# Storing computed data from GpSimd, loading in program order in the last phases, and moving first sums and gate rows a little

## The chip, the cores and the metric

The kernel runs on one core of a Trainium2 chip. The time is the device time of one execution in microseconds (us), as the median of several runs. The core has five engines with instruction queues of their own: TensorE (PE: matmuls, and PEld for its weight loads), VectorE (DVE), ScalarE (ACT), GpSimd (POOL) and SyncE (SP). Each works its queue in order. A transfer (DMA) is started by an instruction in one engine's queue, which waits there until the data or the buffer it needs is ready; what stands behind it in that queue waits with it. The instructions themselves signal each other by semaphores.

## What is computed

One layer of a gated hybrid decoder for a prompt of 1024 tokens and 8 samples of 8 tokens, together 1088 rows. The model width is 1024, everything is float32.

```python
h = rmsnorm(x, norm_g) * (1.0 + scale[:, None]) + shift[:, None]     # shift, scale, gate = split(silu(c) @ ada_w + ada_b)
z = h @ w_in + b_in                                                   # one projection, 8456 columns, split below
ya, v_rows = chunk_gmlp(a_u, a_v, gmlp_vnorm_g, gmlp_ws, gmlp_bs)     # branch a: 128-position mixing in 4 channel groups
ya = ya * silu(a_g)
yb = swa_branch(b_q, b_k, b_v, ...) * silu(b_g)                       # branch b: attention over a window of 128
yc = mlstm_branch(c_qk, c_v, c_i, c_f, c_o, ...) * silu(c_g)          # branch c: mLSTM matrix memory, 4 heads
gates = sigmoid(m_g).reshape(bsz, t, 3, 1024)
merged = (gates[:, :, 0] * (ya @ w_branch_a)
          + gates[:, :, 1] * (yb @ w_branch_b)
          + gates[:, :, 2] * (yc @ w_branch_c))
x_out = x + gate[:, None] * (merged @ w_out)
```

It also returns the new key and value windows, the mLSTM states (C, n, m, the convolution's last rows) and the normed values of the gMLP samples.

## The kernel before

Matmuls keep float32 precision by splitting each operand into a high part (a cast on ScalarE to the matmul's type) and a low part (the rest, a subtraction on VectorE), and adding three products: high by high, high by low, low by high. A weight tile is thus loaded by SP, cast on ScalarE (L1377), subtracted on VectorE (L1378), and then used; hh/hl, yh/yl and mh/ml are the high and low parts of h, of a branch's y and of the merged rows.

In time the kernel has these parts. Up to 60 us it loads x and forms h. Up to 364 us it computes branch c (projections, convolution, and per head the mLSTM). Up to 618 us it computes branch b (key and value tiles, then attention steps with other matmuls filled in between) and the gMLP's values and mixing. From 618 to 1118 us comes what is called the gate phase here: the list `items`, worked one after the other, each prepared five items ahead (LEAD = 5; to prepare is to load and split weights). Most items are one of seven products of a Strassen-like scheme (`seven`, order Q7 = 1, 6, 7, 5, 3, 2, 4), which forms four blocks of a 2 x 2 block product out of seven; each product has two banks (j = 0, 1) of 272 columns with twelve matmuls each, and `collect` adds the bank to running sums on VectorE (L1457 to L1492). First come the four groups of branch a's gMLP, with the rows of the adaLN gate (`gate_rows`) between them; then per branch (order a, c, b) four pairs of merge gates and, behind each pair, two projections (`proj`) of the branch's y by its weights. `proj` multiplies the gate's tanh by the bank (L1610), for the second and third branch adds what the branches before left in DRAM (`mprev`, loaded from dmg at L1608, added at L1612), and stores to dmg (L1616); the last branch's last two row blocks (f = 3, 7) stay on the chip. `y_load` (L1573 to L1575) brings a branch's y from DRAM (dy) in eight loads through a staging buffer of two halves, casting and splitting each; it is an item of its own ahead of the first `proj` of branches c and b. `gate_b` multiplies branch b's y by its gate through DRAM.

From 1118 us on, the output projection: gbc and gbs (the adaLN gate, from drow) and six merged row blocks (mgr, from dmg) are loaded, mgr is split, the columns of w_out are loaded in four parts by `wo_load`, and 36 tiles are computed, 128 rows by 256 columns each, four times nine, of which the ninth has the 64 sample rows. Each takes 24 matmuls, then on VectorE the product with the gate (L1747) and the sum with x (L1748; xr, loaded at L1729), and is stored (L1749).

The order of the work: a scheduler places each engine's instructions by a simulation with priorities (`tc.high_priority()`), except where a manual schedule is entered for an engine: there the queue has the order of the program text. PE is in manual order from the kv tiles' end on (L1309). In before, SP is ordered by the scheduler throughout, and nearly all transfers, loads and stores, stand in its queue; POOL computes 32 operations and issues no transfer.

Of the kernel before, what the change touches and what calls it, by code (L numbers as in the profile page):

```python
# [30 lines left out]
HC = HT // 2  # L31
# [8 lines left out]
def trunk_kernel(ctx: ExitStack, tc: tile.TileContext, I, O):  # L40
    nc = tc.nc
# [419 lines left out]
    with tc.tile_pool(name="cph", bufs=1, side="right", reuse_waits="tile") as c1:  # L461
# [48 lines left out]
        for s, hs in ((0, (2, 3)), (1, (0, 1))):  # L510
# [14 lines left out]
            if s == 0:  # L525
# [43 lines left out]
                V.tensor_tensor(mt, cum, MM, ALU.add)  # L569
                nc.sync.dma_start(O["m_p"].rearrange("a b h -> (a h) b"), mt[:, 1023:1024])  # L570
                nc.sync.dma_start(O["m_s"].rearrange("a b h -> (a h) b"), smpl(mt)[:, :, 8])
                mprev = c1.tile([4, 16], F32, name="mprev")
# [28 lines left out]
                scr = dp.tile([8, NT], F32, name="scr")  # L601
                nc.sync.dma_start(scr[0:4], nM)
                nc.sync.dma_start(scr[4:8], wi)
                for q in range(3):
# [21 lines left out]
        hn = [None] * 4  # L626

        def head(h):
# [44 lines left out]
            for g in range(3):  # L673
# [27 lines left out]
                else:  # L701
                    S.copy(num[:, 6:8], pn[:, 0:258].rearrange("p (i x) -> p i x", x=129))
                    S.copy(num[:64, 8], pn[:64, 258:387])
            nc.sync.dma_start(O["C_p"][0, 0, h], Cp[:, 0:128])
            V.tensor_copy(nst[:, 0, h:h + 1], Cp[:, 128:129])
# [13 lines left out]
            for b2 in range(2):  # L719
                bs_ = slice(4 * b2, 4 * b2 + 4)  # L720
                V.tensor_tensor(Cs[b2], Cs[b2], dec[:, bs_].broadcast_to([128, 4, 129]), ALU.mult)
                V.tensor_tensor(vhm[:, bs_], vs.bitcast(F32).unsqueeze(1).broadcast_to([128, 4, 128]),
                                bmask[:, bs_].unsqueeze(2).broadcast_to([128, 4, 128]), ALU.mult)
                vlm = c1.tile([64, 4, 128], F32R, tag="kwm", bufs=2, name="vlm")
                V.tensor_tensor(vlm, vl.unsqueeze(1).broadcast_to([64, 4, 128]),
                                bmask[:64, bs_].unsqueeze(2).broadcast_to([64, 4, 128]), ALU.mult)
                pu = pk()
                mm(pu, kws, vhm[:, bs_].rearrange("p b e -> p (b e)"), True, False)
                mm(pu, kws[:64], vlm.rearrange("p b e -> p (b e)"), False, True)
                V.tensor_tensor(Cs[b2][:, :, 0:128], Cs[b2][:, :, 0:128], pu.rearrange("p (b e) -> p b e", b=4), ALU.add)  # L730
                V.tensor_tensor(Cs[b2][:, :, 128:129], Cs[b2][:, :, 128:129], un[:, bs_].unsqueeze(2), ALU.add)
                nc.sync.dma_start(O["C_s"][0, bs_, h].rearrange("b d e -> d b e"), Cs[b2][:, :, 0:128])
                V.tensor_copy(nst[:, 1 + 4 * b2:5 + 4 * b2, h:h + 1], Cs[b2][:, :, 128:129])
# [45 lines left out]
        V.tensor_copy(nrowo, ps[0:36, 0:128])  # L779
        nc.sync.dma_start(O["n_p"].rearrange("a b h d -> (a b h) d"), nrowo[0:4])  # L780
        nc.sync.dma_start(O["n_s"].rearrange("a b h d -> (a b h) d"), nrowo[4:36])
        crow = c1.tile([27, 1024], F32, tag="acc", name="crow")
        for q in range(2):
# [3 lines left out]
            S.copy(crow[:, 512 * q:512 * q + 512], ps[0:27])  # L787
        nc.sync.dma_start(O["conv_p"].rearrange("a b j c -> (a b j) c"), crow[0:3])
        nc.sync.dma_start(O["conv_s"].rearrange("a b j c -> (a b j) c"), crow[3:27])

        for h in range(4):
# [17 lines left out]
            gemm_T(wview(hl, 0, 128, 1024), wview(hl, 1, 128, 1024), 8, hh, hlo, ev_g)  # L809
            nc.sync.dma_start(dy[0, h], hn[h])  # L810

# [19 lines left out]
    with tc.tile_pool(name="bph", bufs=1, side="right", reuse_waits="tile") as b1:  # L831
# [62 lines left out]
        def spatial(step):  # L894
            ps = pk()
            if step == 0:
# [3 lines left out]
                G.affine_select(WTp, WTp, [[0, 4], [1, 128]], ALU.is_ge, 0.0, base=0, channel_multiplier=-1)  # L900
                nc.sync.dma_start(dWT, WTp)
                return
# [4 lines left out]
            G.affine_select(WTq, WTq, [[0, 4], [8, 8], [0, 8]], ALU.is_ge, 0.0, base=7, channel_multiplier=-1)  # L907
            nc.sync.dma_start(dWs, WTq)


        for nm, src in (("swa_k_s", "cache_swa_k"), ("swa_v_s", "cache_swa_v")):
            nc.sync.dma_start(O[nm][0, :, 0:120].rearrange("b j g d -> b (j g d)"),
                              I[src][0, :, 8:128].rearrange("b j g d -> b (j g d)"))
# [22 lines left out]
        def k_norm(n0):  # L936
# [9 lines left out]
            if n0 == 6:  # L946
                kout = bt([128, 2, 2, 64], "kout", tag="QT", bufs=3)
                V.tensor_tensor(kout.rearrange("p a g d -> p (a g) d"), v[:, 2:6],
                                kgb.unsqueeze(1).broadcast_to([128, 4, 64]), ALU.mult)
                nc.sync.dma_start(O["swa_k_p"][0, 0], kout[:, 0])  # L950
                for b in range(8):
                    nc.sync.dma_start(O["swa_k_s"][0, b, 120:128], kout[8 * b:8 * b + 8, 1])
            V.tensor_tensor(v, v, kqg.unsqueeze(1).broadcast_to([128, 6, 64]), ALU.mult)
# [69 lines left out]
        class Prompt:  # L1023
# [57 lines left out]
            def v(self):  # L1081
                g, n = self.g, self.n
                pO = pu_()
                for w in range(0 if n > 0 else 1, 2):
                    for r in range(2):
# [3 lines left out]
                S.activation(o, pO[:, 0:256], AF.Copy, scale=0.5)  # L1089
                nc.sync.dma_start(dy[1, 2 * g:2 * g + 2, :, 128 * n:128 * n + 128].rearrange("f p t -> p f t"),  # L1090
                                  o.rearrange("p (f t) -> p f t", f=2))
# [5 lines left out]
        class Sample:  # L1097
# [59 lines left out]
            def y(self):  # L1157
# [6 lines left out]
                c0 = 1024 + 32 * self.bg  # L1164
                nc.sync.dma_start(dy[1, 2 * self.g:2 * self.g + 2, :, c0:c0 + 32].rearrange("f p t -> p f t"), o)

        bhl = {}

        def bg_chunk(f, ci):
# [5 lines left out]
            def ev_b(ci, c0, n, ps):  # L1175
# [4 lines left out]
                V.scalar_tensor_tensor(z, t, 1.0, z, ALU.add, ALU.mult)  # L1180
                nc.sync.dma_start(dsg[f, :, c0:c0 + n], z)

# [87 lines left out]
        def mix(g):  # L1270
# [16 lines left out]
            if g == 3:  # L1287
                nc.sync.dma_start(O["gmlp_v_s"][0].rearrange("b t (g c) -> (b t) g c", g=4), A["gvo"])

# [9 lines left out]
        for n in range(9):  # L1299
            kv_tile(hl, n)  # L1300
            if n in (3, 5):
                spatial((n - 3) // 2)
            if n in (1, 3, 5, 7):
                t_first(n // 2)
            if n % 3 == 2:
# [3 lines left out]
        pe.enter_context(tc.manual_schedule(engines={mybir.EngineType.PE}))  # L1309
        nc.sync.dma_start(O["swa_v_p"][0, 0], vB[:, 7])  # L1310
        for b in range(8):
            nc.sync.dma_start(O["swa_v_s"][0, b, 120:128], vB[8 * b:8 * b + 8, 8])
        done = set()
# [275 lines left out]
    def proj(n, f, Tt):  # L1589
# [5 lines left out]
        def run(t):  # L1595
            if n == 2 and f % 4 == 3:
                m_tiles(f)
            for h in range(2):
                for j in range(2):
# [13 lines left out]
                    if n == 2 and f % 4 == 3:  # L1613
                        m_split(f, c0, HC, x)
                    else:
                        nc.sync.dma_start(dmg[f, :, c0:c0 + HC], x)  # L1616

# [4 lines left out]
    def gate_rows(g):  # L1622
# [20 lines left out]
        def run2(_):  # L1643
# [3 lines left out]
            V.tensor_scalar(m, m, 0.5, None, ALU.mult)  # L1647
            nc.sync.dma_start(drow[:, 256 * g:256 * g + 256], m)

# [7 lines left out]
    items += [act(t_in_place, *((k,) for k in range(4)))] + it[0][:5] + it[1][:1] + it[0][5:]  # L1657
    rest = it[1][1:3] + [None] + it[1][3:4] + [None] + it[1][4:5] + [None] + it[1][5:6] + [None] + it[1][6:] + [None]
    rest += it[2][:1] + [None] + it[2][1:2] + [None] + it[2][2:3] + [None] + it[2][3:] + it[3]
    items += [x or gr.pop(0) for x in rest]  # L1660

    def gate_b(f, b):
# [6 lines left out]
        V.tensor_tensor(x, x, y, ALU.mult)  # L1669
        nc.sync.dma_start(dy[1, f, :, c], x)  # L1670

# [13 lines left out]
    def prepare(i):  # L1685
        if i < len(items) and i not in ready:
            with tc.high_priority():
                ready[i] = items[i][0]() if items[i][0] else None

    for i in range(LEAD):  # L1690
        prepare(i)
# [91 lines left out]
```

## Time and profile before

| | before |
|---|---|
| median of 3 runs | 1226.4 us (1224.79 to 1227.68) |
| profiled execution | 1225.66 us |
| its span in the trace | 1223.9 us |
| mean granted TensorE clock | 0.98 |
| branch c | about 60 to 364 us |
| branch b and gMLP mixing | about 364 to 618 us |
| gate phase | about 618 to 1118 us |
| output projection | about 1118 to 1224 us |

A row of the timeline has the start in us, the duration in us, the engine, the line of the kernel, the operation, out<-in with tile names, shapes and a count; in brackets stands how long the engine idled before it and what released it. SPq is SP's queue; its transfers show the time of the issue, not of the data's way. A row of the waits has who waited, for whom, the total in us, how often, and the longest. In a table by stage the columns are the window, its length, and the busy time and count of each engine, then PE's granted clock, the share of the DMA engines and GB/s.

### The profile page before, as it was taken

Reading aid. Unit: us, or ns where it says so; the run is one execution under the profiler, and the core shown is the slowest. Engines: PE = TensorE matmul, PEld = TensorE weight load, DVE = VectorE, ACT = ScalarE, POOL = GpSimd, SP = SyncE. Lnnn points to the kernel's source line nnn. Section 1 sums busy time; section 2 is a strip of 40 time slices with the busy share of each in tenths; the row PEclk is TensorE's granted clock in tenths of the full one; section 3 lists DMA queues with packets and bytes.
Section 4 is the critical chain, followed back from the end, with each engine's and each line's share of the span. In section 5 each row is a group of like instructions: output and inputs, shape, how many; then the busy total and the mean of one; then the engine's idle time right before and its main releaser. Section 6 shows DMA issues by size and latency. Waiting matters only on the chain.

```text
span 1223.9 us, 23322 instructions
## 1 busy us (share of the span) xinstructions
PE 1173.7 (96%) x8900; PEld 1124.1 (92%) x8900; DVE 820.3 (67%) x2146; ACT 485.8 (40%) x1215; POOL 17.8 (1%) x32
## 2 busy tenths in 40 slices
PE   5899999999979999999979999999999999999998
PEld 2689999999969998988878999999999999999998
DVE  4767878655568778886599885655766676668333
ACT  4443444433332266887234433333433342236000
POOL 1000000000001000000000000000000000000000
PEclk9999999999989999999979999999999999999999
DMA  9711222224122211211144246522633364466332
GB/s 328 242 47 36 72 74 70 76 86 126 54 58 67 56 40 44 67 38 59 55 119 118 75 120 201 161 80 84 177 112 110 110 171 125 126 197 190 95 91 83
DMA packets 155818, 129.76 MB, mean 106 GB/s; under 512 B 13551, under 2 KB 146311, under 8 KB 155690
## 3 DMA queue, kind: packets, MB, share of 16 engines
q1 hardware_dynamic: 155706, 128.27, 35.4%
q8 instruction: 70, 1.15, 0.4%
q14 instruction: 42, 0.34, 0.1%
HBM read 99.39 MB, written 29.82 MB: 106 GB/s over the span
## 4 chain that ended last, share of the span: by engine, by line
PE 88%; DVE 5%; SPq 3%; DMA 3%; ACT 1%; issue 1%; DVEq 0%
PE pg L85 48%; PE pk L85 23%; PE pu L85 14%; PE pk L89 2%; DMA raw<-in_w_in_dram 2%; SPq L256 1%; PE pu L89 1%; DMA xts<-in_x_sample_dram 1%; SPq L272 1%; DVE comb L1372 0%; DVE prod L1378 0%; DVE hl L125 0%; ACT hl L124 0%; DVE wo L1378 0%; DVE ml L1585 0%
## 5 line engine op out<-in xcount | busy, mean ns | idle before, releaser
L85 PE MATMUL pg<-hl,hl 128*128 128x256 f32 (+3 forms) x904 | 281.1, 311 | 0.0
L85 PE MATMUL pg<-hh,hl 128*128 128x384 f32 (+1 forms) x912 | 242.2, 340 | 1.1 <-DVE hh L399 1.1
L85 PE MATMUL pg<-hl,hh 128*128 128x256 f32 (+1 forms) x1008 | 182.9, 287 | 1.0 <-DVE zif L524 1.0
L85 PEld LDWEIGHTS pg<-hl,hl 128*128 128x128 f32 x904 | 172.1, 190 | 2.4 <-issue 1.9
L85 PEld LDWEIGHTS pg<-hh,hl 128*128 128x128 f32 x912 | 163.8, 191 | 5.3 <-DVE hh L399 2.2
L85 PEld LDWEIGHTS pg<-hl,hh 128*128 128x128 f32 x1008 | 152.9, 190 | 1.5 <-PE pg L85 1.1
L1377 ACT CAST prod<-raw 128x512 fp32r<-128x512 f32 x76 | 47.1, 620 | 125.7 <-PE pk L85 54.8
L85 PE MATMUL pg<-hh,prod 128*128 128x272 f32 x400 | 84.9, 292 | 6.8 <-ACT prod L1377 6.8
L85 PE MATMUL pk<-hh,prod 128*128 128x272 f32 x368 | 78.0, 291 | 0.0
L85 PEld LDWEIGHTS pg<-hh,prod 128*128 128x128 f32 x400 | 66.7, 191 | 7.3 <-ACT prod L1377 6.9
L1378 DVE TENSOR_TENSOR prod<-raw,prod 128x512 fp32r<-128x512 f32 x76 | 52.0, 686 | 25.2 <-ACT prod L1377 24.9
L1377 ACT CAST prod<-comb 128x512 fp32r<-128x512 f32 x64 | 39.4, 616 | 69.3 <-PE pk L85 29.5
L1502 ACT ACTIVATE tt<-tt,bh 128x272 f32<-128x272 f32 x96 | 49.9, 522 | 41.0 <-DVE tt L1475 15.8
L85 PEld LDWEIGHTS pk<-hh,prod 128*128 128x128 f32 x368 | 61.4, 191 | 1.3 <-issue 0.4
L85 PE MATMUL pk<-tc,prod 128*128 128x272 f32 x444 | 61.5, 287 | 0.0
L85 PE MATMUL pg<-yh,prod 128*128 128x272 f32 x288 | 60.0, 287 | 0.0
L85 PE MATMUL pk<-yh,prod 128*128 128x272 f32 x288 | 59.9, 287 | 0.0
L85 PEld LDWEIGHTS pk<-tc,prod 128*128 128x128 f32 x444 | 57.6, 188 | 0.9 <-DVE tt L1544 0.4
L85 PE MATMUL pg<-hl,prod 128*128 128x272 f32 x200 | 58.1, 291 | 0.0
L85 PE MATMUL pg<-tc,prod 128*128 128x272 f32 x408 | 56.5, 287 | 0.0
L85 PE MATMUL pk<-hl,prod 128*128 128x272 f32 x184 | 53.5, 291 | 0.4 <-DVE hl L825 0.4
L85 PE MATMUL pu<-hh,prod 128*128 128x272 f32 x256 | 53.5, 289 | 0.0
(521 smaller groups left out, 2626.1 us busy)
## 6 DMA issues: line engine op xcount, KB each, us to landing
raw<-in_w_in_dram SPq DMA_DIRECT2D x124, 256.0 KB
dmg<-tt SPq DMA_DIRECT2D x88, 136.0 KB
mprev<-dmg SPq DMA_DIRECT2D x64, 136.0 KB
adaraw<-in_ada_w_dram SPq DMA_DIRECT2D x16, 512.0 KB
stage<-dy SPq DMA_DIRECT2D x24, 272.0 KB
xt<-in_x_prompt_dram SPq DMA_DIRECT2D x8, 512.0 KB
graw<-in_ada_w_dram SPq DMA_DIRECT2D x16, 256.0 KB
raw<-in_w_out_dram SPq DMA_DIRECT2D x32, 128.0 KB
```

Source lines behind the costliest of these rows:

```text
L85: T.matmul(out, lhsT=lhsT, rhs=rhs, start=start, stop=stop)
L89: T.transpose(out, in_, ident[:k, :k])
L256: nc.sync.dma_start(raw.rearrange("p (k c) -> p k c", k=4), kv(ada_w[:, base:base + 256])[:, 4 * (q % 2):4 * (q % 2) + 4])
L272: nc.sync.dma_start(xx[:TILES[n][1]], x_p[128 * n:128 * n + 128] if n < 8 else x_s)
L1377: S.copy(t[:, 0], x)
L1378: V.tensor_tensor(t[:, 1], x, t[:, 0].bitcast(F32), ALU.subtract)
L1502: S.activation(x, x, AF.Tanh, bias=bh[:, b:b + 1], scale=0.5)
```

## The change

It has four parts.

1. Stores of computed data (25 lines of the program, among them dmg, dy, dsg, drow, the scratch rows of branch c, its states and the caches' copies from DRAM to DRAM) are issued from GpSimd's queue instead of SP's. The 36 stores of the output tiles stay on SP, as do all loads.
2. Ahead of the gate phase's loop (line 1690 of the changed kernel) SP enters a manual schedule, so from there to the end its queue has the order of the program. Lines below are one higher in the changed kernel than before (L1608 and L1616 are the same, L1718 is L1719, L1729 is L1730, L1749 is L1750).
3. The four `t_first` sums stand behind kv tiles 5 to 8 instead of 1, 3, 5 and 7.
4. `gate_rows` items stand one place later among the gMLP products.

```diff
-                nc.sync.dma_start(scr[0:4], nM)
+                nc.gpsimd.dma_start(scr[0:4], nM)
...
-            if n in (1, 3, 5, 7):
-                t_first(n // 2)
+            if n > 4:
+                t_first(n - 5)
...
-                        nc.sync.dma_start(dmg[f, :, c0:c0 + HC], x)
+                        nc.gpsimd.dma_start(dmg[f, :, c0:c0 + HC], x)
...
-    rest = it[1][1:3] + [None] + it[1][3:4] + [None] + it[1][4:5] + [None] + it[1][5:6] + [None] + it[1][6:] + [None]
-    rest += it[2][:1] + [None] + it[2][1:2] + [None] + it[2][2:3] + [None] + it[2][3:] + it[3]
+    rest = it[1][1:4] + [None] + it[1][4:5] + [None] + it[1][5:6] + [None] + it[1][6:] + [None]
+    rest += it[2][:1] + [None] + it[2][1:2] + [None] + it[2][2:3] + [None] + it[2][3:4] + [None] + it[2][4:] + it[3]
...
-        nc.sync.dma_start(dy[1, f, :, c], x)
+        nc.gpsimd.dma_start(dy[1, f, :, c], x)
...
+    pe.enter_context(tc.manual_schedule(engines={mybir.EngineType.SP}))
     for i in range(LEAD):
         prepare(i)
```

The queues show what moves. A row has the line, the operation, out<-in, the shape, and a count where rows repeat.

The first place is the step from branch b to the gate phase. SP's queue before, where graw are weights of the adaLN gate and raw those of the first products:

```order
L1628 DMA graw<-in_ada_w_dram 128x2x256 x3
L1367 DMA raw_7314<-in_w_in_dram 128x4x128
L1367 DMA raw_7316<-in_w_in_dram 128x4x128
L1367 DMA raw_7318<-in_w_in_dram 128x4x128
L1628 DMA graw<-in_ada_w_dram 128x2x256
```

and after:

```order
L1251 DMA bsb<-in_gmlp_bs_dram 128x512
L1367 DMA raw_7316<-in_w_in_dram 128x4x128
L1367 DMA raw_7318<-in_w_in_dram 128x4x128
L1367 DMA raw_7320<-in_w_in_dram 128x4x128
L1367 DMA raw_7322<-in_w_in_dram 128x4x128
L1367 DMA raw_7369<-in_w_in_dram 128x4x128
```

The raws now stand ahead of graw, eight of them. On VectorE at this place, after:

```order
L825 TENSOR_TENSOR tc<-tx,tc 128x272 x3
L1517 TENSOR_TENSOR tx<-hh_438,hh_274 128x544
L1518 TENSOR_TENSOR tx<-hl_439,hl_275 128x544
L1519 TENSOR_TENSOR tx<-tx 128x544
L1378 TENSOR_TENSOR prod<-raw_7316,prod 128x512
L825 TENSOR_TENSOR hl_275<-tx,hh_274 128x544
```

The low part of the first weights (L1378) has three sums of `t_in_place` ahead of it.

The second place is `y_load` of branch c. SP's queue after, ahead of branch c's first projections:

```order
L1367 DMA raw_10216<-in_w_branch_c_dram 128x4x128
L1367 DMA raw_10255<-in_w_branch_c_dram 128x4x128
L1367 DMA raw_10290<-in_w_in_dram 128x4x128
L1367 DMA raw_10292<-in_w_in_dram 128x4x128
L1367 DMA raw_10294<-in_w_in_dram 128x4x128
L1367 DMA raw_10296<-in_w_in_dram 128x4x128
L1573 DMA stage<-dy 128x544 x8
L1608 DMA mprev<-dmg 128x272 x8
```

The eight stage loads stand together behind the weights; before, they stood one by one between loads and stores, the first two far ahead. VectorE's order in the seven products ahead of the first projection, before:

```order
L1610 SCALAR_TENSOR_TENSOR tt<-tt,pu 128x272
L1575 TENSOR_TENSOR yl<-stage,yh 128x544
L1610 SCALAR_TENSOR_TENSOR tt<-tt,pg 128x272
L1575 TENSOR_TENSOR yl<-stage,yh 128x544
L1378 TENSOR_TENSOR prod<-raw_9931,prod 128x512
L1575 TENSOR_TENSOR yl<-stage,yh 128x544
```

and after:

```order
L1475 TENSOR_TENSOR tt<-pu,tt 128x272
L1476 TENSOR_TENSOR tt<-pu,tt 128x272
L1575 TENSOR_TENSOR yl<-stage,yh 128x544 x2
L1475 TENSOR_TENSOR tt<-pg,tt 128x272
L1476 TENSOR_TENSOR tt<-pg,tt 128x272
L1378 TENSOR_TENSOR prod<-raw_10290,prod 128x512
L1488 TENSOR_TENSOR tt<-pk,tt 128x272
L1488 TENSOR_TENSOR tt<-pu,tt 128x272
L1378 TENSOR_TENSOR prod<-comb,prod 128x512
L1457 TENSOR_TENSOR tt<-pg,tt 128x272
L1575 TENSOR_TENSOR yl<-stage,yh 128x544
```

The first split of y (L1575) stood among the last projections (L1610) of branch a; it now stands behind the sums on the q = 5 bank (L1475, L1476), and the third behind the first sum of the q = 2 bank (L1457).

The third place is the end. SP's queue before, with w_out, the merged rows and the gate rows between the last projections' mprev:

```order
L1718 DMA raw_13464<-in_w_out_dram 128x256 x2
L1718 DMA raw_13470<-in_w_out_dram 128x256
L1705 DMA mgr<-dmg 128x1088 x4
L1718 DMA raw_13470<-in_w_out_dram 128x256
L1718 DMA raw_13476<-in_w_out_dram 128x256 x2
L1705 DMA mgr<-dmg 128x1088 x2
L1699 DMA gbc<-drow 128x1024
L1701 DMA gbs<-drow 8x1024 x8
```

and after:

```order
L1608 DMA mprev<-dmg 128x272 x8
L1700 DMA gbc<-drow 128x1024
L1702 DMA gbs<-drow 8x1024 x8
L1706 DMA mgr<-dmg 128x1088 x6
L1719 DMA raw_13460<-in_w_out_dram 128x256 x2
...
L1719 DMA raw_13503<-in_w_out_dram 128x256 x2
L1730 DMA xr<-in_x_prompt_dram 128x256
L1750 DMA out_dram<-oo 128x256
L1730 DMA xr<-in_x_prompt_dram 128x256
L1750 DMA out_dram<-oo 128x256
```

All of gbc, gbs, mgr and the 16 first loads of w_out stand behind the last mprev, and the first xr behind them. In the tiles, xr and the store of a tile alternate in both; before, two xr stood ahead of the first store, so that each xr was one tile ahead of its use, and after, each stands behind the store of the tile before.

44 lines of the change are left out of this document (22 added, 22 removed).

## The prediction

> **What bounds the kernel now.** I read the page first (busy shares, chain), then busy time by stage, then the waits, then the timeline at the three places where the order on SyncE (SP in the profile) changes.
>
> ```profile
> span 1223.9 us, 23322 instructions
> PE 1173.7 (96%) x8900; PEld 1124.1 (92%) x8900; DVE 820.3 (67%) x2146; ACT 485.8 (40%) x1215; POOL 17.8 (1%) x32
> PE 88%; DVE 5%; SPq 3%; DMA 3%; ACT 1%; issue 1%; DVEq 0%
> ...
> core 0: us, PE busy (x) PEld busy (x) DVE busy (x) ACT busy (x) POOL busy (x), PEclk, DMA share, GB/s
> 618.00:640.00 22.00, 15.16 (x99) 14.59 (x99) 20.48 (x38) 9.10 (x18) 0.00 (x0) 0.76 0.52 144
> 640.00:1110.00 470.00, 469.57 (x3763) 464.09 (x3762) 317.17 (x661) 169.77 (x326) 0.00 (x0) 1.00 0.45 132
> 1110.00:1224.00 114.00, 108.21 (x900) 107.61 (x898) 49.10 (x115) 12.77 (x30) 0.00 (x0) 0.98 0.37 108
> ```
>
> TensorE (PE) is busy 96% of the span and is 88% of the chain that ended last. By stage the margin is plain: in the gate phase, 640 to 1110 us, PE works 469.57 of 470.00 us at clock 1.00. There is nothing there to gain, and whatever makes PE wait there is lost in full. What is left to gain near the change is the 22 us after 618 us, where PE is busy only 15.16 us at clock 0.76.
>
> ```profile
> SPq L1616 <- DVE tt L1612: 72.5, 51, 8.1
> ```
>
> This row is SP's own queue: 72.5 us in 51 waits for VectorE (DVE), because a store to dmg holds everything behind it. That is what the change takes away, but SP's waits are no one's loss while PE stands still for none of them. So I price the change by who sets PE's waits after it.
>
> **a. The step from the B branch to the gate phase.**
>
> ```profile
> 619.44 0.43 PE L85 MATMUL pk<-WTs,vn 64*128 64x64 f32 x2
> ...
> 619.90 1.40 SPq L1628 DMA_DIRECT2D graw<-in_ada_w_dram  x3
> 621.34 1.68 SPq L1367 DMA_DIRECT2D raw<-in_w_in_dram  x3
> 625.96 0.62 ACT L1377 CAST prod<-raw 128x512 fp32r<-128x512 f32 x1 [1.24 <-DMA raw<-in_w_in_dram]
> 626.63 0.59 PE L85 MATMUL pg<-hh,prod 128*128 128x272 f32 x1 [6.76 <-ACT prod L1377]
> 626.79 0.69 DVE L1378 TENSOR_TENSOR prod<-raw,prod 128x512 fp32r<-128x512 f32 x1
> ```
>
> SP issues nothing until PE's last mix (619.44 + 0.43) has ended, because graw, which takes memory that the mixing reads, stands ahead of the first raw; PE then idles 6.76 us. In program order the raws come first and don't wait for that mix; they are there long before 620. What is late next is DVE: in the new order the low part of the first weights (L1378) stands behind the three sums L1517 to L1519 and comes at about 624.0 to 624.7, and PE needs it for its third product, which ran at 627.5. So PE goes on about **2.8 us** earlier (627.5 - 624.7). Bounds: the whole 6.76, and 0 if DVE is later still.
>
> **b. y_load, twice (branches c and b).** It brings the branch's y from DRAM in 8 loads through two staging halves, so load n+2 waits until DVE has split load n.
>
> ```profile
> 776.01 0.42 SPq L1573 DMA_DIRECT2D stage<-dy  x1
> ...
> 859.00 0.32 SPq L1573 DMA_DIRECT2D stage<-dy  x1
> 861.72 0.65 ACT L1574 CAST yh<-stage 128x544 fp32r<-128x544 f32 x1 [0.79 <-DMA stage<-dy]
> ...
> 863.05 1.66 PE L85 MATMUL pu<-tc,prod 128*128 128x272 f32 x12
> 871.59 0.71 DVE L1575 TENSOR_TENSOR yl<-stage,yh 128x544 fp32r<-128x544 f32 x1
> 875.05 0.28 PE L85 MATMUL pu<-yh,prod 128*128 128x272 f32 x1
> 876.43 0.29 PE L85 MATMUL pu<-yh,prod 128*128 128x272 f32 x1
> ```
>
> Before, the first load goes at 776.01, some 78 us ahead of the branch, and the last split (871.59) is done 3.5 us before PE's first use (875.05). After, all eight stand behind four weight loads of the next seven products. In the times of before: a bank takes 1.5 us (863.05 to 875.05 are eight). DVE's order puts split 1 behind the two sums on the first q=5 bank, which is complete at 863.05 + 1.66 = 864.7, with three weight sums ahead of them: split 1 is done by about 866.6 and load 3 goes. Split 3 stands behind the sum on the first q=2 bank, four banks on (870.7), and is done by 871.9; load 5 goes at 872.1. Split 5 stands behind L1492 of the last q=4 bank, seven banks on (875.2), and a weight sum: done by 876.7; load 7 goes. From issue to cast a load takes 2.72 us (859.00 to 861.72), cast and split 0.65 and 0.71: split 7 is done at 880.8. PE's first bank needs it for its last three products, which ended at 876.7 (876.43 + 0.29): 880.8 + 0.4 = 881.2, a stall of 4.5 us, in steps, and PE at a lower clock afterwards. The next two rows have the same 24 matmuls at the start of the last phase, behind gaps of 1 to 2 us, and when it runs freely:
>
> ```profile
> 1124.00 4.15 PE pu L85 x24
> 1133.59 2.72 PE pg L85 x24
> ```
>
> That is 1.4 us more. So 2 x (4.5 + 1.4) = **+11.8**. Bounds: 0, if DVE's splits go ahead of its sums, and 20, if each step of the relay slips by a sum.
>
> **c. The start of the output projection.**
>
> ```profile
> 1090.89 1.77 SPq L1705 DMA_DIRECT2D mgr<-dmg  x4
> 1098.30 8.10 SPq L1701 DMA_DIRECT2D gbs<-drow  x8
> 1114.43 0.43 DVE L1612 TENSOR_TENSOR tt<-tt,mprev 128x272 f32<-128x272 f32 x1
> ...
> 1098.00:1102.00 4.00, 4.00 (x34) 4.00 (x33) 4.00 (x9) 3.20 (x7) 0.00 (x0) 1.00 1.01 364
> 1118.31 0.40 PE L85 MATMUL pk<-prod,mh 128*128 128x256 f32 x2
> ```
>
> Before, SP sends the merged rows (mgr), and w_out with them, over 20 us ahead of their first use at 1118.31. After, they stand behind the eight mprev of the last projections, and mprev 8 waits for the buffer that DVE gives free with the fifth sum, at about 1114.9 (1114.43 + 0.43). Then gbc, eight gbs (0.27 us each if nothing holds them: 2.6 us with their gaps; the row above, 8.10 us, is the other end), and mgr from 1118.9. Six times 544 KB are 3.34 MB; at the 364 GB/s of that row and the 403 of the four us before it, 8.3 to 9.2 us, so the last lands near 1128 to 1130, the first w_out right behind. Then a cast (1.1), a split (1.28) and the weights' split (0.68): PE has its operands at about 1132, 14 us late, but in one piece where tiles 0 and 1 of before went in steps. Tile 0 takes 4.2 us at the low clock, its two DVE steps 0.85, and its xr stands behind the 16 w_out loads, whose five buffers free up only as DVE splits them: the first store goes at about 1139.3 against 1128.05: **+11.3** (bounds +6, +18: gbs at 8.1, a slower stream).
>
> **d. The 36 output tiles.** The output stores stay on SP, and with SP in program order each xr load stands behind the store of the tile before, which waits for that tile's last DVE step.
>
> ```profile
> 1128.05 0.34 SPq L1749 DMA_DIRECT2D out_dram<-oo  x1
> 1128.49 0.38 SPq L1729 DMA_DIRECT2D xr<-in_x_prompt_dram  x1
> 1131.37 0.42 DVE L1748 TENSOR_TENSOR oo<-oo,xr 128x256 f32<-128x256 f32 x1
> ...
> 879.71 0.43 SPq L1608 DMA_DIRECT2D mprev<-dmg  x1
> 881.93 0.44 DVE L1612 TENSOR_TENSOR tt<-tt,mprev 128x272 f32<-128x272 f32 x1 [0.25 <-DMA mprev<-dmg]
> 1218.37 3.21 SPq L1749 DMA_DIRECT2D out_dram<-oo  x2
> ```
>
> Before, one xr is always ahead, and a tile takes PE's 2.72 us. After, it is a ring: add done to store next to nothing, store to xr 0.44 (1128.05 to 1128.49), xr to data, add 0.42. For xr to data I take 2.22 us: the mprev load, 136 KB behind a 136 KB store, on which DVE waits at 881.93. The sum is **3.1 us a tile**, more than PE's 2.72. PE runs ahead by up to eight banks, then waits. 35 periods of 3.08 are 108 us; ahead of tiles 9 and 18 stand eight w_out loads each, 8 x 0.45 plus half a microsecond in which xr lands behind them, 8 us for both: 116, against 93.2 before (1128.05 to the last store, 1221.2): **+23**. Bounds: 0, if xr lands within 1.8 us, and +40, if it takes the 2.7 of the larger stage load.
>
> **Edits at nothing.** The stores on GpSimd (POOL): SP's 0.32 us an issue goes, and POOL, busy 17.8 us in all, has room; its price for one has no row, so the bounds are -3 to +5, the lower end from freer loads in the B phase, the upper because in the C branch POOL's selects now stand behind four stores a head. t_first later: DVE has slack; bounds -2.3 to 0. Gate rows a place later: PE's count is the same, its cover the bank of the product beside it; without that cover 0.5 each.
>
> The Trainium skill, "SBUF — State Buffer", section "Who interferes with whom", speaks against the first edit: GpSimd writes a DMA's descriptors through a port pair that DVE's copies and casts lock for a whole instruction, and the store waits. Its figure would be some 2.5 us on a store of 0.6; I estimate from it nothing at all for this kernel's sum, since a dmg store is read again only by the next branch, or by mgr, and DVE's rows in these phases are sums, which the page excepts. No trace here shows a store from GpSimd.
>
> **The sum.** The profiled execution took 1225.66 us, 1.8 over its span and 0.7 below the median of 1226.4. 1225.7 - 2.8 + 11.8 + 11.3 + 23 = 1269.0; I give **1269**.
>
> **Rivals.** (1) *The ring is hidden*: xr lands within 1.8 us, the period is at PE's 2.72, and d falls to about 1. Then 1225.7 - 2.8 + 11.8 + 11.3 + 1 = 1247. For it: the last phase moves only 108 GB/s, and 2.22 us was taken where the queue carried the gate phase's 132. Against it: 0.3 less would only bring the ring to PE's pace. Chance 0.25; b at half puts it at 1241. (2) *Everything slips more*: gbs at 8.1 us each time and a ring of 3.5: 1269 + 5 + 15 = 1289. Chance 0.1. (3) *Faster*: SP, freed of 72.5 us of waits, runs so far ahead that b, c and d find their data ready, as SP's windows before would have allowed without the dmg stores; then only a is left, with all its 6.76 us and the 2.3 us of t_first: 1216 to 1223. It decides at mprev: SP must pass the last mprev before 1095 or so, when mgr went before. Against it stands the buffer: mprev has three, and the eighth is free only when the fifth is added, 1114.8. Chance 0.07. (4) *It doesn't do what it says*: the stores move but the loads are as early as before; then nothing beyond a: within 0.2% (which is about what a measurement can tell from no change). Chance 0.04.
>
> **How the numbers follow.** My forecast, with d at its value, holds 0.54, from 1250 to 1282. Range 1240 to 1286: it takes in rival 1 with b at half and most of rival 2; what is left out is 0.2. Faster by over 0.2%: 0.07; within 0.2%: 0.04; slower: 0.89.
>
> **What would show it.** Right: PE's gap at 620 shrinks to about 4 us; at the first projection of branches c and b PE waits some 4 us for DVE L1575; PE waits 12 to 14 us for mgr or w_out near 1118; in the last phase DVE's add waits for DMA xr each tile, and the stores are 3.1 us apart. Wrong: stores 2.7 us apart (then rival 1), PE without waits at the first projection (b is nothing), mgr issued before 1100 (c is nothing), or PE waiting in the C branch for POOL's select.

## The result and the profile after

| | before | changed |
|---|---|---|
| median | 1225.6 us | 1302.3 us |
| lowest to highest of 4 runs each | 1222.8 to 1227.7 | 1296.4 to 1306.3 |
| profiled execution, its span | 1225.66, 1223.9 us | 1296.4, 1294.7 us |
| mean granted TensorE clock | 0.98 | 0.962 |

The changed kernel takes 1.0624 times as long (95% interval 1.0574 to 1.0673). The sign was forecast, with three of the four places; the sizes were not: 77 us instead of 43, and above the range.

The page of the changed kernel, its busy times, chain and queues:

```profile
PE 1181.5 (91%) x8900; PEld 1128.3 (87%) x8900; DVE 822.1 (63%) x2146; ACT 485.2 (37%) x1215; POOL 119.9 (9%) x211
...
q0 software_dynamic: 9008, 25.38, 5.4%
...
PE 72%; DMA 12%; DVE 7%; issue 3%; SPq 3%; ACT 2%; POOL 0%; DVEq 0%; POOLq 0%; ACTq 0%
```

The work is the same (8900 matmuls, 1181.5 us against 1173.7), but TensorE's share of the chain fell from 88% to 72%, and transfers rose from 3% to 12%. The q0 row is new: 25.38 MB of stores that GpSimd issues. GpSimd's own instructions have 0% of the chain; one of its stores stands in it all the same, as shown below. The waits of the changed kernel say who stands for whom:

```profile
DVE oo L1749 <- DMA xr<-in_x_prompt_dram: 77.1, 29, 4.0
...
PE pk L85 <- ACT prod L1377: 15.9, 1, 15.9
...
PE pu L85 <- ACT yh L1574: 6.5, 4, 2.8
...
PE pg L85 <- DVE prod L1378: 2.6, 1, 2.6
...
PE pk L85 <- ACT hh L824: 2.1, 1, 2.1
```

From the top: the ring of the output tiles (d), their start (c), y_load (b), and two waits of the gate phase's first 30 us (a). Where the two profiled executions part is read from the same instruction in both (the end of the last mix; the sum L1610 on the last projection bank of branch a, and on the fourth bank of the first projection of branches c and b; the first and the last output store):

| stretch, up to | before | changed | added there | forecast |
|---|---|---|---|---|
| last mix ends (all before the gate phase) | 619.87 | 622.38 | +2.5 | 0 |
| branch a's last projection (a) | 854.45 | 858.56 | +1.6 | -2.8 |
| branch c's first projection (b) | 881.25 | 893.38 | +8.0 | +5.9 |
| branch b's first projection (b) | 1013.38 | 1031.65 | +6.1 | +5.9 |
| first output store (c) | 1128.05 | 1161.48 | +15.2 | +11.3 |
| last output store (d) | 1221.2 | 1291.7 | +37.1 | +23 |

The sum is 70.5 us. The profiled execution was the fastest of the four; the median is 6 us above it.

**Ahead of the gate phase.** Timeline of the changed kernel at the last mixes, and at the end one row of its chain:

```profile
608.91 2.58 SPq L1367 DMA_DIRECT2D raw<-in_w_in_dram  x5
610.66 0.72 POOL L1165 DMA_DIRECT2D dy<-ys  x1 [3.94 <-ACT ys L1162]
...
615.40 0.44 DVE L1230 TENSOR_TENSOR tx<-hh,tc 128x272 f32<-128x272 f32 x1 [3.00 <-DMA dy<-ys]
...
617.62 1.33 PE L85 MATMUL pk<-WT,vn 128*128 128x128 f32 x8 [1.68 <-DVE sA L1278]
...
619.69 2.08 PE L85 MATMUL pk<-WT,vn 128*128 128x128 f32 x8 [0.74 <-DVE sA L1278]
...
610.66 4.62 DMA dy<-ys
```

The first five raws now go before the mixing has ended, and a store of branch b's y (dy, from the tile ys) that GpSimd issues among them takes 4.62 us to land; the two such stores before it took 1.97 and 1.95. VectorE's next sum (L1230), whose buffer comes from the same five as ys, waits for it, and TensorE waits 1.68 and 0.74 us for VectorE: these 2.4 us are nearly all of the first row of the table. From 580 to 610 us the two executions are level to 0.3 us.

**Step d.** Timeline of the changed kernel in the tiles, SyncE's queue and VectorE's sum with x:

```profile
1204.64 0.42 DVE L1749 TENSOR_TENSOR oo<-oo,xr 128x256 f32<-128x256 f32 x1 [2.56 <-DMA xr<-in_x_prompt_dram]
1205.09 0.34 SPq L1750 DMA_DIRECT2D out_dram<-oo  x1
1205.48 0.43 SPq L1730 DMA_DIRECT2D xr<-in_x_prompt_dram  x1
1207.94 0.42 DVE L1749 TENSOR_TENSOR oo<-oo,xr 128x256 f32<-128x256 f32 x1 [2.54 <-DMA xr<-in_x_prompt_dram]
1208.39 0.34 SPq L1750 DMA_DIRECT2D out_dram<-oo  x1
```

This is the ring: sum, store, load, and VectorE idle until the load is there. From issue to use xr takes 2.46 us (1205.48 to 1207.94), a turn 3.30; the median of the 35 distances between stores is 3.34. Where a column of w_out changes, the chain shows another wait in it:

```profile
1192.81 2.95 DMA raw<-in_w_out_dram
1195.86 0.63 ACT wo L1377
1196.51 0.69 DVE wo L1378
1197.29 0.44 DVE oo L1749
```

VectorE's sum stands in its own order behind the split of the weights just loaded. The two distances there are 8.04 and 7.84 us.

**Step c.** Timeline around the end of the gate phase:

```profile
1128.96 4.74 SPq L1608 DMA_DIRECT2D mprev<-dmg  x4
1133.75 1.76 SPq L1700 DMA_DIRECT2D gbc<-drow  x1
1135.56 3.96 SPq L1702 DMA_DIRECT2D gbs<-drow  x8
1139.69 3.14 SPq L1706 DMA_DIRECT2D mgr<-dmg  x6
...
1150.97 1.10 ACT L1584 CAST mh<-mgr 128x1088 fp32r<-128x1088 f32 x1
1151.98 0.61 ACT L1377 CAST prod<-raw 128x512 fp32r<-128x512 f32 x1
...
1152.65 0.58 PE L85 MATMUL pk<-prod,mh 128*128 128x256 f32 x1 [15.95 <-ACT prod L1377]
...
1159.97 0.69 DVE L1378 TENSOR_TENSOR wo<-raw,wo 128x512 fp32r<-128x512 f32 x1 [0.87 <-ACT wo L1377]
1160.58 0.42 DVE L1748 TENSOR_TENSOR oo<-pk,gbc 128x256 f32<-128x256 f32 x1
```

SyncE comes past the last mprev only at 1133.7, and everything follows in its order. ScalarE then takes the six merged blocks ahead of the first weights, and TensorE starts after 15.95 us, at half its pace (0.58 us for a matmul that takes 0.28 when running freely). Its first tile is complete at 1158.69 us, but VectorE's product with the gate comes only at 1160.58, behind the weights' splits of the next columns.

**Step b.** TensorE at the first projection of branch c, and the eight loads on SyncE:

```profile
866.45 16.95 SPq L1573 DMA_DIRECT2D stage<-dy  x8
...
884.97 0.60 PE L85 MATMUL pu<-yh,prod 128*128 128x272 f32 x1 [2.82 <-ACT yh L1574]
...
885.00:891.00 6.00, 5.84 (x24) 5.53 (x25) 2.98 (x6) 0.65 (x1) 0.91 (x2) 0.50 0.43 136
```

The relay takes 17 us of SyncE's queue, and TensorE waits at the fourth part, as drawn in the prediction. All its waits there are 3.9 us at branch c and 3.7 at branch b; the rest of the 8.0 and 6.1 us is the low clock behind them, 0.50 in the window of the last row.

**Step a.** TensorE behind the last mix, and 25 us later, with two windows:

```profile
623.73 0.60 PE L85 MATMUL pg<-hh,prod 128*128 128x272 f32 x1 [1.35 <-ACT prod L1377]
627.18 0.82 PE L85 MATMUL pg<-hh,prod 128*128 128x272 f32 x2 [2.63 <-DVE prod L1378]
...
650.65 0.39 PE L85 MATMUL pk<-hh,prod 128*128 128x272 f32 x1 [2.07 <-ACT hh L824]
652.04 0.39 PE L85 MATMUL pk<-hl,prod 128*128 128x272 f32 x1 [0.99 <-DVE hl L825]
...
622.00:650.00 28.00, 22.59 (x155) 21.87 (x154) 27.49 (x52) 11.83 (x24) 0.00 (x0) 0.82 0.24 66
650.00:660.00 10.00, 8.36 (x52) 8.15 (x53) 8.46 (x20) 4.16 (x9) 0.00 (x0) 0.83 0.00 1
```

The third product runs 4.8 us after the mix (622.38 to 627.18) where it took 7.7 before: the 2.8 us were won, through the wait that the prediction named. At 650 they were lost again: the last block of t_in_place is late, and the clock in the second window is 0.83 (1.00 before). VectorE is busy 27.49 of the 28 us up to there.

### The profile page after: what moved, and what is told of

The parts are those of the page before. It is cut to its first block, busy times and chain, and to the rows that moved or that the text cites. A ratio compares the mean times of both kernels' runs of the same rounds, so it can differ in the third digit from the quotient of the medians.

```text
span 1294.7 us, 23488 instructions
## 1 busy us (share of the span) xinstructions
PE 1181.5 (91%) x8900; PEld 1128.3 (87%) x8900; DVE 822.1 (63%) x2146; ACT 485.2 (37%) x1215; POOL 119.9 (9%) x211
## 3 DMA queue, kind: packets, MB, share of 16 engines
q0 software_dynamic: 9008, 25.38, 5.4%
## 4 chain that ended last, share of the span: by engine, by line
PE 72%; DMA 12%; DVE 7%; issue 3%; SPq 3%; ACT 2%; POOL 0%; DVEq 0%; POOLq 0%; ACTq 0%
PE pg L85 39%; PE pk L85 19%; PE pu L85 11%; DMA xr<-in_x_prompt_dram 5%; PE pk L89 2%; DMA raw<-in_w_in_dram 1%; SPq L256 1%; DMA xts<-in_x_sample_dram 1%; DVE oo L1748 1%; DMA xr<-in_x_sample_dram 1%; DMA xt<-in_x_prompt_dram 1%; DMA out_dram<-Cs 1%; PE pu L89 1%; DVE oo L1749 1%; DMA stage<-dy 1%
## 5 line engine op out<-in xcount | busy, mean ns | idle before, releaser
L1378 DVE TENSOR_TENSOR prod<-raw,prod 128x512 fp32r<-128x512 f32 x76 | 51.9, 688 | 32.8 <-ACT prod L1377 32.8
L1749 DVE TENSOR_TENSOR oo<-oo,xr 128x256 f32<-128x256 f32 (+1 forms) x36 | 15.3, 424 | 86.8 <-DMA xr<-in_x_prompt_dram 77.1
L1616 POOL DMA_DIRECT2D dmg<-tt x88 | 47.7, 542 | 244.7 <-DVE tt L1612 215.3
```

Source lines behind the costliest of these rows:

```text
L1378: V.tensor_tensor(t[:, 1], x, t[:, 0].bitcast(F32), ALU.subtract)
L1616: nc.gpsimd.dma_start(dmg[f, :, c0:c0 + HC], x)
L1749: V.tensor_tensor(ot[:tn], ot[:tn], xr[:tn], ALU.add)
```

## The experiments

Each run is timed beside the kernel before on the same chip; that one had medians of 1225.6 to 1226.9. "Won" is against the 1302.3 of the changed kernel.

### E1: SyncE ordered by the scheduler again

```diff
-    pe.enter_context(tc.manual_schedule(engines={mybir.EngineType.SP}))
```

> The changed kernel without the manual schedule of SyncE; stores on GpSimd, later first sums and gate rows stay. Theory (the program order of SyncE costs nearly all): b, c and d go, some 66 of the 71 us, and the time is 1225 to 1235. Rival (stores issued by GpSimd are slow and hold those who wait for the data): most of the loss stays, 1270 or more. Between the two, the rest over 1226 is what the stores and the moved sums cost.

Measured: 1231.35 us, 1.0041 times before (1.0029 to 1.0054). 71 of the 77 us are SyncE's program order; the stores on GpSimd and the moves leave 5.7.

### E2: x loaded two tiles ahead

```diff
-            nc.sync.dma_start(xr[:tn], (x_p[t0:t0 + 128, c] if n < 8 else x_s[:, c]))
+            xr_load(xq[0] + 2)
+            xr = xrs.pop(xq[0])
```

> The changed kernel with x's tiles (xr) loaded two tiles ahead in the program, nothing else. Theory (d is a ring through the store's place in SyncE's queue): the tiles run at TensorE's 2.7 us, the 130 us from first to last store fall to 93 to 98, the time to about 1267 (-35). Rival (the tiles are slow for another reason, as slower transfers or VectorE's order): less than 10 us are gained.

Measured: 1266.59 us, 35.7 won. From the first store to the last it is 93.4 us (1170.8 to 1264.2), as before. The window of the tiles in this run:

```profile
1170.00:1266.00 96.00, 93.24 (x794) 93.04 (x793) 36.54 (x84) 6.45 (x12) 0.00 (x0) 1.00 0.36 112
```

TensorE doesn't wait in it, and its clock is 1.00. The ring is d, all of it: the two turns at the column changes are still 8.40 and 7.73 us in this run, but now turns of 0.92 to 2.37 behind them catch up, since the next xr are there already.

### E3: gbc, gbs, mgr and the first w_out ahead of the last two projections

```diff
+        if i == len(items) - 2:
+            start_out()
         items[i][1](ready.pop(i))
...
-    nc.sync.dma_start(gbc, drow[0:1].broadcast_to([128, 1024]))
...
-    wo_load(0)
```

> The changed kernel with gbc, gbs, mgr and the first quarter of w_out loaded ahead of the last two projections in the program. Theory (c is the place of these loads behind the last mprev): TensorE's wait of 15.9 us ahead of the first tile falls under 2, the time by 13 to 16 us, to about 1288. Rival (the loads wait for something else, as the stores of dmg from GpSimd to land): the wait stays over 8 us.

Measured: 1290.96 us, 11.3 won, a little less than expected. TensorE's longest wait in this run between 1115 and 1162 us:

```profile
PE pk L85 <- ACT mh L1584: 1.5, 1, 1.5
```

The wait of 15.9 us is gone; the data was never held by the stores from GpSimd.

### E4: y_load ahead of the seven products

```diff
+            if p == 0 and n:
+                items.append((None, lambda _, n=n: y_load(n)))
             gate_pair(ORDER_BR[n], p, Tt)
-            if p == 0 and n:
-                items.append((None, lambda _, n=n: y_load(n)))
```

> The changed kernel with y_load as the item ahead of the branch's first seven products instead of behind them. Theory (b is the place of the eight loads in SyncE's queue and of the splits in VectorE's): both stalls at a branch's first projection go, 12 to 14 us are gained, the time is about 1289. Rival (the relay of eight loads through two halves just moves, and holds the weights behind it): 0 to 5 us.

Measured: 1285.43 us, 16.9 won; TensorE has no wait at all between 850 and 1060 us. The 2.8 us beyond the 14.1 of the table lie within the changed kernel's own spread of 10 us.

### F1 and F2: the moves alone, the stores alone

F1 is the kernel before with

```diff
-            if n in (1, 3, 5, 7):
-                t_first(n // 2)
+            if n > 4:
+                t_first(n - 5)
```

and the gate rows a place later; F2 is the kernel before with all 25 lines of `nc.gpsimd.dma_start`.

> The kernel before with only the moved first sums and gate rows (edits 3 and 4). E1 left 5.7 us over the kernel before that SyncE's program order does not explain. Theory (the stores on GpSimd cost them, above all up to 620 us): this run is within 2 us of 1225.6. Rival (the moves cost them, as VectorE's work before the gate phase comes late): 1229 to 1232.

> The kernel before with only the stores issued from GpSimd (edit 1). Theory (they cost the 5.7 us of E1): 1229 to 1232, with the loss ahead of 620 us. Rival (the moves cost them): within 2 us of 1225.6, or faster if a SyncE freed of the 72.5 us of waits is worth something by itself.

Measured: F1 1227.13 us, 1.0011 (0.9995 to 1.0027), not told from no change. F2 1232.23 us, 1.0051 (1.0034 to 1.0067): the stores alone cost as much as E1's 5.7 us.

### F3 and F4: all three places repaired

F3 is the changed kernel with the edits of E2, E3 and E4. F4 has these and SyncE's program order too, but of the stores only the gate phase's three lines (dmg, drow and gate_b's dy) on GpSimd, and no moves.

> The changed kernel with the three repairs of E2, E3 and E4 together. Theory (the three losses stand one after the other on TensorE's path and add): 1302.3 - 35.7 - 11.3 - 16.9 = 1238.4, between 1235 and 1242, so program order of SyncE then costs some 7 us beside E1. Rival (they overlap or hide one another): above 1245, or below 1230.

> The kernel before with GpSimd only for the stores of the gate phase (dmg, drow, dy of gate_b), SyncE in program order from there on, and the three repairs; the earlier stores stay on SyncE, sums and gate rows stay where they were. Theory (the loss of E1 lies in the earlier stores, and the raws ahead of graw are worth 2.6 us at most): 1223 to 1230. Rival (program order costs by itself even when its three places are repaired): 1231 or more.

Measured: F3 1235.08 us, 67.2 won, where the three alone won 63.9 together: they add, within the runs' spread. F4 1231.09 us, 1.0046 (1.0030 to 1.0062), at the rival's edge: program order with the three repairs costs some 4 us more than H2 below, which has the same stores on GpSimd. The two profiles part by 2.5 us from the last mix to the end of branch a's projections, 2.9 in the two stretches of y_load and 0.8 up to the first output store; the tiles are 2.3 faster.

### H1 and H2: which stores cost

H1 is F2 with

```diff
-            nc.gpsimd.dma_start(O[nm][0, :, 0:120].rearrange("b j g d -> b (j g d)"),
+            nc.sync.dma_start(O[nm][0, :, 0:120].rearrange("b j g d -> b (j g d)"),
```

H2 is the kernel before with only the gate phase's three lines on GpSimd.

> The kernel of F2 (all stores of computed data on GpSimd, else as before) with the two copies of the attention caches, DRAM to DRAM, back on SyncE, where they go some 46 us later. Theory (the copies at the start take bandwidth from the loads that the first 60 us wait for): 2 to 4 us faster than F2's 1232.2, and TensorE's first transposes of x_sample at about 59 us as before, not 61 to 63. Rival (the loss lies in the stores of branch c or of the gate phase): within 1 us of F2.

> The kernel before with GpSimd only for the stores of the gate phase (dmg, drow, dy of gate_b), all of SyncE by the scheduler. Theory (F2's loss lies ahead of the gate phase, and SyncE's waits for dmg cost TensorE nothing): 1224 to 1227, the same as before; F4's 1231.1 then holds some 5 us that program order costs even when its three places are repaired. Rival (the GpSimd stores of the gate phase cost F4 its 5 us): 1229 to 1232.

Measured: H1 1227.23 us, 1.0012 (0.9997 to 1.0028), 5.0 below F2, more than expected. H2 1227.22 us, 1.0016 (1.0001 to 1.0031). So the two copies of the attention caches, DRAM to DRAM, are most of what the stores cost in F2. In F2 their issue and TensorE's work in the second 10 us are:

```profile
L912 POOL DMA_DIRECT2D out_dram<-in_cache_swa_k_dram x1: 684/684/684, 1.6 to 1.6; - x1
...
10.00:20.00 10.00, 4.07 (x27) 1.36 (x27) 7.24 (x35) 3.45 (x6) 0.00 (x0) 1.00 1.02 344
```

and in H1:

```profile
L912 SPq DMA_DIRECT2D out_dram<-in_cache_swa_k_dram x1: 746/746/746, 47.9 to 47.9; - x1
...
10.00:20.00 10.00, 7.56 (x59) 2.98 (x63) 5.93 (x28) 3.27 (x6) 2.10 (x1) 0.97 1.10 376
```

GpSimd has nothing to do at 1.6 us and sends them at once, 960 KB in front of the loads for which TensorE waits; SyncE sent them at 48 us. TensorE is busy 4.07 of those 10 us instead of 7.56. Its first transposes of x_sample come at 61.49 us in F2 and at 59.00 in H1 (58.95 before), so 2.5 of the 5.0 us are seen by then; where the others lie isn't shown. One trace is weak evidence here: F1, which leaves the copies in place, has 61.41 in its profile, the slowest of its twelve runs.

### H3: the output stores on GpSimd too

```diff
-            nc.sync.dma_start(O["y_p"][0, t0:t0 + 128, c] if n < 8 else
+            nc.gpsimd.dma_start(O["y_p"][0, t0:t0 + 128, c] if n < 8 else
```

> The changed kernel with the 36 output stores issued from GpSimd too, so that nothing on SyncE stands between one xr and the next. Theory (d is the store ahead of xr in one queue): as E2, 1264 to 1269, with the stores 2.7 us apart. Rival (a store from GpSimd takes longer to land or to be issued, and the tiles slow down, or the end is late by it): above 1271.

Measured: 1267.49 us, 34.8 won, as E2. The ring is cut as well by taking the store out of the queue as by taking the load ahead of it.

### H4: two blocks' sums on GpSimd

```diff
-        V.tensor_tensor(x, x, y, ALU.add)
+        W = G if k > 1 else V
...
+        W.tensor_tensor(x, x, y, ALU.add)
```

> The changed kernel with the sums of t_in_place for its third and fourth block computed on GpSimd instead of VectorE, nothing else. Theory (what was won at 627 us is given back at 650 us, because VectorE, full from 618 to 650, brings the last block of the q=7 product late): TensorE's waits of 2.1 and 1.0 us at 650 go, with the low clock behind them, and 3 to 5 us are gained: about 1298. Rival (the block is late because its one buffer is handed from block to block, or GpSimd's sums take longer): the waits stay or grow, and nothing is gained.

Measured: 1300.78 us, 1.5 won, within the spread; TensorE's waits at the block grew to 0.5 and 3.4 us. This is as its rival forecast, but it doesn't decide between the theories, because it slowed VectorE itself. VectorE and GpSimd in this run:

```profile
637.13 0.68 DVE L1378 TENSOR_TENSOR prod<-comb,prod 128x512 fp32r<-128x512 f32 x1
638.09 1.50 DVE L1378 TENSOR_TENSOR prod<-comb,prod 128x512 fp32r<-128x512 f32 x1
639.51 1.84 DVE L1378 TENSOR_TENSOR prod<-raw,prod 128x512 fp32r<-128x512 f32 x1
...
639.00 1.80 POOL L1519 TENSOR_TENSOR tx<-hl,hl 128x544 f32<-128x544 f32 x1
```

A subtraction of 0.68 us takes 1.50 and 1.84 while GpSimd adds. Not each one does: the first ran while GpSimd's sum from 636.75 on took 2.29 us, where the same sum took 1.36 at 645.86.

### K1, K2 and K3: the step from the mix to the gate phase by itself

K1 is F1 with SyncE in program order over the first eight items only, so that the raws stand ahead of graw. K2 is the changed kernel with the first gate row item ahead of group 0's q=7 product; K3 is both on F1.

```diff
+    with tc.manual_schedule(engines={mybir.EngineType.SP}):
...
-    items += [act(t_in_place, *((k,) for k in range(4)))] + it[0][:5] + it[1][:1] + it[0][5:]
+    items += [act(t_in_place, *((k,) for k in range(4)))] + it[0][:5] + it[1][:1] + [gr.pop(0)] + it[0][5:]
```

> The kernel before with the moved sums and gate rows and with SyncE in program order only over the gate phase's first items, so that the raws stand ahead of graw; no other place is in program order and no store is moved. Theory (step a is right at 627 us and given back at 650): TensorE's third product comes 4.8 us after the last mix and not 7.7, but it waits 2 to 4 us at the last block of the first q=7 product; the time is 1224 to 1229, as F1's 1227.1. Rival (the give-back comes from elsewhere in the changed kernel): 1222 to 1225, without a wait at 650.

> The changed kernel with the first gate row item ahead of group 0's q=7 product, so that TensorE has other work while VectorE finishes the last block. Theory (VectorE brings that block late): the waits of 2.1 and 1.0 us shrink by the 1.7 us of the gate row's 16 products or go, with the low clock behind them; 2 to 4 us are gained, about 1299. Rival (graw comes too late there, TensorE waits for it instead): no gain.

> K1 with the first gate row item ahead of group 0's q=7 product. Theory: what step a wins is kept, 2 to 4 us below K1, 1221 to 1225, and so below the kernel before if anything here is. Rival (as for K2): as K1.

Measured: K1 1227.48 us, 1.0009 (0.9998 to 1.0021); K2 1297.45 us, 4.9 won; K3 1225.87 us, 1.0002 (0.9991 to 1.0013). K1 has both sides of step a without the rest of the change:

```profile
623.73 0.82 PE L85 MATMUL pg<-hh,prod 128*128 128x272 f32 x2 [3.40 <-DVE prod L1378]
...
646.78 0.39 PE L85 MATMUL pk<-hh,prod 128*128 128x272 f32 x1 [2.08 <-ACT hh L824]
648.17 0.59 PE L85 MATMUL pk<-hl,prod 128*128 128x272 f32 x1 [0.99 <-DVE hl L825]
```

The mix ends there at 617.76, so the third product comes 6.0 us after it (7.7 before; I had expected 4.8), and the 2.1 and 1.0 us at the last block are there to within a hundredth. In K2 and K3 the first of them is 0.9 and the second still 1.0. From the last mix to the end of branch a's projections it is 234.6 us before, 236.2 in the changed kernel, 237.1 in K1, 234.9 in K2 and 235.9 in K3: earlier weights lose 1.6 to 2.5 us, and work put in front of the late block gets 1.2 to 1.3 of it back. The sign doesn't hang on one trace: E2, E3, E4 and H3, with the changed kernel's program up to there, have 236.3 to 236.4, and the kernels without the early weights 234.3 to 235.3. Of K2's 4.9 us in the medians only these 1.3 are seen at the place.

None of the fifteen kernels beats the kernel before by more than the runs can tell; K3, expected at 1221 to 1225, is level with it.

## Why the prediction was right in its places and wrong in its sizes

- **What bounds the kernel** stood: a wait of TensorE in the gate phase was lost in full, each of the three repairs gave its piece back, and they added (63.9 apart, 67.2 together).
- **d failed by its size, and about half of the miss is here**: 37.1 us, not 23, which is 14.1 of the 27.2 us by which the table's sum is above the forecast's 43.3. The ring is as drawn, but "For xr to data I take 2.22 us" was mis-sized: 2.46, from a load of another tile behind another store. Over 35 turns the period of 3.34 instead of 3.08 makes 9 us. The w_out loads at the column changes were put at 8 us together and cost 9.2 over two turns (8.04 and 7.84, less 3.34 each), since VectorE's sum also waits there behind the weights' split, a wait that I had not named. The remaining 4 us are single turns, the longest of 4.0 to 4.8. The bound of +40 for d held it; the forecast and the range's end of 1286 leaned on the mprev row.
- **c** was 15.2, not 11.3, within its bounds (+6, +18). SyncE passed the last mprev where I put it (1114.9 and the 18.3 us added by then make 1133.2; it was 1133.7). Three steps then follow. From the end of VectorE's fifth sum to the first mgr it took 6.3 us (1133.35 to 1139.69), where the prediction has 4.0 (1114.9 to 1118.9): gbc and gbs were mis-sized. From there to TensorE's start it took 13.0 us (to 1152.65), as the prediction has it (1118.9 to 1132). From TensorE's start to the first store it took 8.8 us, not 7.3: the product of the first tile stood behind the weights' splits of the next columns, a wait that I had not named.
- **b** was 14.1, not 11.8: the relay as worked out, the waits 3.9 and 3.7 us where the prediction has 4.5, most of them for the cast (L1574) and not for the split (L1575). The clock behind them, 1.4 us each in the prediction, was mis-sized: it cost 4.1 and 2.4. A slip without weight in the sum: 871.59 is where before's last split starts; it is done at 872.30, 2.75 us ahead of its use and not 3.5.
- **a failed as a step**: -2.8 was right at 627 us and is shown by the trace, but the prediction stopped at the next wait. VectorE was the bound from 618 to 650 us (20.48 of 22 us busy in the row that the prediction quoted, 27.49 of 28 in the changed kernel's), so earlier weights could not bring its last block earlier: from its first sum (L1517) to the last block's low part (L825) it needs 26.5 us before (621.93 to 648.47) and 26.9 in the changed kernel (624.40 to 651.26). TensorE ran ahead into it, waited 3.1 us and lost clock. K1 shows this by itself, and K2 and K3 agree, where work in front of the block shrinks the wait; no run takes work off VectorE without slowing it.
- **The stretch ahead of the gate phase** was put at nothing, and cost 2.5 us in the profiled execution. It takes both parts of the change together: the raws that no longer wait for the mixing, and a store issued by GpSimd among them. In all eight kernels with both (the changed one, E2, E3, E4, F3, H3, H4, K2) that store took 4.2 to 4.8 us to land, and TensorE waited 1.8 to 3.2 us for VectorE's L1278; in E1, F2 and H1, with the store on GpSimd and the raws later, it took 1.95 to 1.96, and TensorE waited 1.3 us or less. In F4, K1 and K3 the store is on SyncE and the raws go behind it; TensorE's waits there are 0.9 us or none. No run tests this alone.
- **The stores on GpSimd**, put at nothing with bounds -3 to +5, cost 6.6 by F2 against its own before (1232.23 and 1225.68), above the bound of +5. The reason given for the upper end, selects behind stores, is not it: H1 puts 5.0 of it on the two cache copies, whose new place at 1.6 us I passed over. H2, the gate phase's stores alone, is 1.0016. The port rule of the Trainium skill ("SBUF — State Buffer", "Who interferes with whom"), which I weighed at nothing for these stores, is needed for none of the waits found here: GpSimd's 36 output stores in H3 had landed in a median of 2.2 us, and the ring was cut.
- **The moves** were put at nothing, and F1 (1.0011) can't tell them from nothing.
- **The rivals**: the hidden ring (1247) is refuted by E2. The faster one needed SyncE past the last mprev before 1095; it was there at 1133.7. The second, everything slips more, came nearest with 1289; its ring of 3.5 us was near the 3.34 measured, but its gbs of 8.1 us took 3.96, and it had no loss before the gate phase. The fourth, that the loads stay as early as before, is refuted by SyncE's times in all three places.
- The rest: the changed kernel's runs reach from 1296.4 to 1306.3, and the median's 6 us above the profiled execution are not located. In the profiles of E2, E3 and E4, the slowest executions of those kernels, the last mix ends near 630 us, in H3's, near its median, at 628.2, and not at 622.4, with the same program up to there. But in F1's, with no store on GpSimd, it ends at 624.8, and in H2's, with none there up to this point, at 617.5: up to there executions differ by several us without the change, so what part of the 6 us is the change's isn't shown.

## What to carry to other kernels

A queue put in program order makes each load wait for whatever the program puts ahead of it: walk the program once per queue, and where a load follows a store of a result, write the ring with the load's own way from issue to use and compare it with the other engine's pace, at both ends of what that way may be. A wait that is taken away counts only up to the next engine that is full: read on until that engine has slack. And an idle engine that is given a transfer sends it at once, so look at what it then stands in front of. Two moves that are cheap apart can meet: loads sent earlier stood in the way of a store that another engine's buffer waited for.

## What had not been expected of the hardware

- VectorE's two-input subtraction, 0.68 us, took 1.50 to 1.84 us while GpSimd ran two-input sums (H4). The Trainium skill, "SBUF — State Buffer", section "Who interferes with whom", says that a two-input VectorE instruction contends with GpSimd's reads; this run agrees, with a factor of 2.2 to 2.7, though not for each instruction that overlaps.
- With waits of 2.1 and 1.0 us in them, 10 us (650 to 660) had a granted clock of 0.83; behind 3.9 us of waits at branch c's first projection it was 0.50 from 885 to 891 us; after 15.95 us without work a matmul of 0.28 us took 0.58.
- A store from GpSimd that landed 1.96 and 1.95 us after its issue in E1 and F2 took 4.2 to 4.8 us where SyncE issued five loads of 256 KB around it.
- GpSimd's issue of an output store took 0.54 us (median in H3) where SyncE's took 0.34.
